# Two query tiles as one seven-product pair job ahead of the gate pair jobs, in a streaming-encoder layer on one core

## The chip, the cores and the metric

The kernel runs on one core of a Trainium2 chip as one program. The metric is the device time of one execution in microseconds, given as a median of runs. A core has five engines that run side by side, each in its own program order: TensorE (PE, matrix products; its weight loads are shown apart as PEld), VectorE (DVE), ScalarE (ACT), GpSimd (POOL) and SyncE (SP, which here only issues DMAs). They wait for one another by semaphores.

## The reference

One layer with four parts: a gated feed-forward, a mixing part with two branches, and a second gated feed-forward, with RMS norms around each. The change lies in the mixing part, whose core is

```python
u = rms_norm(h, mix_pre_g[l])
q, k, v, xr, xg = jnp.split(u @ w_in[l], splits, axis=-1)
xr = causal_conv(xr, conv_w[l], conv_b[l])
hr = rg_lru(xr, rg_a_w[l], rg_a_b[l], rg_x_w[l], rg_x_b[l], lru_lambda[l])
y_a = (hr * jax.nn.gelu(xg)) @ w_lru_out[l]
y_b = swa_sink_attention(q, k, v, attn_sinks[l], bias) @ w_attn_out[l]
g = jax.nn.sigmoid(u @ w_gate[l] + b_gate[l]).reshape(b, s, N_BRANCHES, d)
merged = g[:, :, 0] * y_a + g[:, :, 1] * y_b
```

There are 512 tokens and 1024 channels; q has 1024 columns (16 heads of 64), xg has 1024. `rg_lru` ends in a scan over the tokens; the attention needs q, k and v.

## The kernel before

**Precision by parts.** Every fp32 operand is held as a high part, which ACT makes by a copy into a reduced type, and a low part, the difference that DVE makes. A product is three matmuls: high by high, low by high, high by low. Weights come in by SP's queue as raw tiles of 512 KB; `split_to` or `split2` makes the parts. Tiles come from one pool of 42 slots (`NSLOT`); a tile that is asked for while none is free waits for the last reader of an old one.

**Plain units.** `unit(nm, i)` makes 128 output features for all 512 tokens: `mm_feat` (lines 216 to 227) issues 24 matmuls of 512 columns into one PSUM bank. Its weights are asked for by `get`, which splits two tiles ahead and loads three further ones; this running ahead ends where tiles of pair jobs begin (the set `paired`).

**Pair jobs.** `Pairs` makes two feature tiles at once, by seven products in place of eight (a scheme of Strassen's kind, in Winograd's form). The weights of two tiles are quartered into a11, a12, a21 and a22; POOL makes the sums s1, s2 (in tile S12) and s3, s4 (S34). The inputs' quarter sums t1 to t4 are made once. A job is seven blocks (`mm_s`, lines 485 to 496) of 12 matmuls with 256 columns, over four k-tiles. `prep(m, i)` readies job m's weights in five steps: 0 POOL's sums, 1 the parts of a11 and a12, 2 of s12, 3 of s34, 4 of a22. In `GeluPairs.run` (line 644) the blocks are issued in the order a11, s1, [a22 of the job before], s2, a12, s4, s3; the last job issues a12 after s3, then its own a22. Three banks are used per job: `bu` by a11, s2, s3 and a22, which add up in it with ACT copying the state between them (q1 after a11, line 658; u after s2; v after s3, line 682); `bx` by s1 and s4; `bc` by a12. Preparation of the next job stands between the blocks, as do `last` (the gelu of the quarter that a22 closes), `mult` (line 698, times the scan's result) and `parts` (the high and low parts of the product, yh and yl, inputs of the later `lru` units).

**What sets the order.** Each engine's instructions are laid down by hand in program order. `point()` (line 201) moves a counter on by one; `later(n, fn, rank)` puts work n points ahead, and at each point the work that has come due is issued, lower rank first. `mm_feat` calls `point` twice per unit, each value tile once, `mm_s` once per block. `point(True)` issues all that is still waiting.

**The stage of the change.** In order: units xr 4 to 7 (points 1 to 8), wg 0 to 7 (9 to 24), wk 0 and 1 (25 to 28), four value tiles (29 to 32), wq 0 and 1 (33 to 36), `point(True)`, then four xg pair jobs, then units mixed with the attention's steps (`att_units`, from line 1377 on). Between them stand, by points: the recurrent branch's gates, decay factors (`rg_decay`) and scans (`rg_scan`, line 1133: eight square roots on ACT at `SCAN_AT`, then the scan of tile i on DVE `SCAN_LAG[i]` points later, a product and a scan); the first pair job's preparation (`PREP_AT`, its raw loads and those of the second job at `RAW_AT`, the second job's sums at `PREP_1`). `k_out` (line 1207) takes the keys from PSUM: four ACT copies, two DVE differences, two ACT copies across. `v_out` makes the parts of the values. `q_out` (line 1244) takes a query tile from PSUM: two ACT copies of 64 rows with the scale, then two DVE differences, into a QS tile whose upper rows hold the high part and whose lower rows the low part. `att_s` (line 1278) multiplies QS 2g and 2g + 1 by the keys of group g. `t_spill` writes t1 to t4 to memory through SP's queue, in xg jobs 1 and 2, for a later stage.

Of the kernel before, what the change touches and what calls it, by code (L numbers as in the profile page):

```python
# [13 lines left out]
ALU = mybir.AluOpType  # L14
# [37 lines left out]
def hybrid_layer(ctx: ExitStack, tc: tile.TileContext, a: dict, out: bass.AP):  # L52
# [68 lines left out]
    order += [("wk", 0), ("wk", 1), ("wv", 0), ("wv", 1)]  # L121
    order += [("wq", 0), ("wq", 1)]
    paired.update(range(len(order), len(order) + 8))
    order += [("xg", i) for i in range(8)]

# [71 lines left out]
    def later(n, fn, rank=1):  # L197
        uid[0] += 1
        due.append((now[0] + n, rank, uid[0], fn))
# [29 lines left out]
    def unit(nm, i, **kw):  # L229
        w = get(nm, i)  # L230
        ps = bank("f")
        mm_feat(ps, w, **kw)
        return ps
# [407 lines left out]
    class GeluPairs(Pairs):  # L641


        def run(self, scans, yh, yl, tail, between):
            X, end = self.X, len(self.jobs) - 1
# [5 lines left out]
            for n, (nm, f) in enumerate(self.jobs):  # L651
# [32 lines left out]
                if n == end:  # L684
                    c11()
                gelu(c[:, 0, :])
                if n < end:
# [3 lines left out]

                def last(W=W, bu=bu, c=c):
                    mm_s(W["a22"], X["t4"], bu, True)
                    act.activation(c[:, 1, :256], bu, AF.Gelu_apprx_tanh)
                    gelu(c[:, 1, 256:])

                def mult(c=c, f=f):
                    dve.tensor_tensor(out=c, in0=c, in1=scans[f // 2], op=ALU.mult)

                def parts(c=c):  # L700
                    yh.append(slot([P, 2, SEQ], F32R, name="yh"))
                    yl.append(slot([P, 2, SEQ], F32R, name="yl"))
                    split2(yh[-1], yl[-1], c)
# [441 lines left out]
    X3 = {"b11": uview(0, 0), "b21": uview(1, 0), "b22": uview(1, 1)}  # L1145
    pairs_g = GeluPairs(("xg",), 0, 8, X3)

    def t_hi(key, src):
# [103 lines left out]

    for i in range(2):
        ps = unit("wq", i)
        later(1, lambda i=i, ps=ps: q_out(i, ps))

    yh, yl = [], []
    point(True)
    spills = {1: ("t1", "t2"), 2: ("t3", "t4")}
    pairs_g.run(scans, yh, yl, lambda: split_to(st["split"] + 1), lambda n: [t_spill(key) for key in spills.get(n, ())])  # L1260
    X3 = pairs_g = None
# [211 lines left out]
SCAN_AT = (23,) * 8  # L1473
SCAN_LAG = (1, 2, 3, 4, 5, 6, 7, 8)

T_AT = (3, 4, 5, 6), (4, 5, 6, 7)
RAW_AT = (18, 27)
PREP_AT = (22, 27, 29, 31, 33)
PREP_1 = 30
NSLOT = 42  # L1480
# [70 lines left out]
```

## Time and profile before

| what | value |
|---|---|
| time, median of 3 runs | 1128.34 us (1128.21 to 1128.47) |
| profiled execution, its own time | 1128.54 us |
| its span, first to last instruction | 1126.8 us |
| mean granted TensorE clock | 0.998 |
| HBM read, written | 121.74 MB, 11.53 MB |
| instructions | 18041 |

The profile is of one execution. Its page gives busy times for each engine, the span in 40 slices, the chain of work that ended last, and the costliest groups of instructions. A timeline row has the start, the duration, the engine, the line in the kernel, the operation, out<-in by the program's names, shapes and count, and in brackets the idle time of the engine before it with what ended it. Starts are in us from the span's start.

### The profile page before, as it was taken

To read this page: it belongs to the slowest core of one execution; us is meant where nothing else is said; L and a number is where in the kernel's file an instruction comes from. 1 tells how busy PE (TensorE), PEld (TensorE's weight loads), DVE (VectorE), ACT (ScalarE), POOL (GpSimd) and SP (SyncE) were. 2 spreads that over 40 slices of the span, in tenths; PEclk is the share of its full clock that TensorE was granted. 3 is DMA by queue.
4 is the path that set the end of the run, shared out by engine and by line. 5 is a ranking of instruction groups with operands and counts; after the bars stand their busy time and mean duration, and the time that the engine had idled before them with its cause. 6 is when DMAs were issued, how large, how long until landed. Compare 5 with 4: busy or idle time off the path is not lost.

```text
span 1126.8 us, 18041 instructions
## 1 busy us (share of the span) xinstructions
PE 1118.7 (99%) x7018; PEld 1012.3 (90%) x7018; DVE 833.1 (74%) x1233; ACT 620.8 (55%) x1107; POOL 362.0 (32%) x282
## 2 busy tenths in 40 slices
PE   9999999999999999999999999999999999999997
PEld 8899999988889977899888888889999999998886
DVE  5889989886436998887778867767898777975313
ACT  7755555574325788756655654456555555564211
POOL 0044344200000523232656663000866566700000
PEclk9999999999999999999999999999999999999999
DMA  9226563265213553156132336521333232264101
GB/s 346 96 86 148 133 133 113 76 224 164 98 57 139 164 116 105 38 165 247 57 94 75 131 112 225 180 101 38 113 105 93 103 113 87 87 203 167 38 20 56
DMA packets 40310, 136.54 MB, mean 121 GB/s; under 512 B 4880, under 2 KB 6800, under 8 KB 40224
## 3 DMA queue, kind: packets, MB, share of 16 engines
q1 hardware_dynamic: 36432, 123.28, 32.4%
q0 software_dynamic: 3504, 11.58, 5.2%
q8 instruction: 55, 0.90, 0.3%
q10 hardware_dynamic: 288, 0.52, 0.1%
q14 instruction: 31, 0.25, 0.1%
HBM read 121.74 MB, written 11.53 MB: 118 GB/s over the span
## 4 chain that ended last, share of the span: by engine, by line
PE 99%; DVE 0%; issue 0%; DVEq 0%; POOL 0%; ACT 0%; POOLq 0%
PE c L492 13%; PE c L493 13%; PE c L494 13%; PE f L223 9%; PE f L224 9%; PE f L225 9%; PE acc L243 8%; PE acc L241 8%; PE acc L242 8%; PE pt L1329 1%; PE s L1293 1%; PE s L1292 1%; PE tr L333 1%; PE o L1345 1%; PE o L1346 1%; PE f L847 1%
## 5 line engine op out<-in xcount | busy, mean ns | idle before, releaser
L493 PE MATMUL c<-uT,wlo 128*128 128x256 f32 x516 | 146.0, 283 | 0.0
L494 PE MATMUL c<-uT,whi 128*128 128x256 f32 x516 | 146.0, 283 | 0.0
L492 PE MATMUL c<-uT,whi 128*128 128x256 f32 x516 | 146.0, 283 | 0.0
L493 PE MATMUL c<-Xh,wlo 128*128 128x256 f32 x504 | 142.7, 283 | 0.0
L492 PE MATMUL c<-Xh,whi 128*128 128x256 f32 x504 | 142.7, 283 | 0.0
L223 PE MATMUL f<-uT,whi 128*128 128x512 f32 (+1 forms) x392 | 140.6, 359 | 0.0
L224 PE MATMUL f<-uT,wlo 128*128 128x512 f32 (+1 forms) x392 | 139.1, 355 | 0.0
L225 PE MATMUL f<-uT,whi 128*128 128x512 f32 (+1 forms) x392 | 139.0, 355 | 0.0
L241 PE MATMUL acc<-whi,hT 128*128 128x512 f32 x352 | 137.1, 390 | 0.0
L242 PE MATMUL acc<-wlo,hT 128*128 128x512 f32 x352 | 137.0, 389 | 0.0
L243 PE MATMUL acc<-whi,hT 128*128 128x512 f32 x352 | 136.9, 389 | 0.0
L214 DVE TENSOR_TENSOR wlo<-S,whi 128x1024 fp32r<-128x1024 f32 x86 | 126.7, 1473 | 7.5 <-POOL OL L1365 4.5
L494 PE MATMUL c<-Xl,whi 128*128 128x256 f32 x456 | 129.0, 283 | 0.0
L213 ACT ACTIVATE whi<-S 128x1024 fp32r<-128x1024 f32 x86 | 88.3, 1054 | 23.7 <-DVE S L539 22.0
L493 PEld LDWEIGHTS c<-uT,wlo 128*128 128x128 f32 x516 | 99.0, 192 | 0.2
L492 PEld LDWEIGHTS c<-uT,whi 128*128 128x128 f32 x516 | 99.0, 192 | 0.2
L494 PEld LDWEIGHTS c<-uT,whi 128*128 128x128 f32 x516 | 99.0, 192 | 0.0
L492 PEld LDWEIGHTS c<-Xh,whi 128*128 128x128 f32 x504 | 96.8, 192 | 0.3 <-issue 0.3
L493 PEld LDWEIGHTS c<-Xh,wlo 128*128 128x128 f32 x504 | 96.7, 192 | 0.1
L494 PEld LDWEIGHTS c<-Xl,whi 128*128 128x128 f32 x456 | 87.5, 192 | 0.0
L223 PEld LDWEIGHTS f<-uT,whi 128*128 128x128 f32 x392 | 74.1, 189 | 11.6 <-issue 1.6
L225 PEld LDWEIGHTS f<-uT,whi 128*128 128x128 f32 x392 | 74.1, 189 | 10.5
(380 smaller groups left out, 2858.5 us busy)
## 6 DMA issues: line engine op xcount, KB each, us to landing
raw_w2a<-in_w2a_dram SPq DMA_DIRECT2D x22, 512.0 KB, 4.0
raw_w1b<-in_w1b_dram SPq DMA_DIRECT2D x22, 512.0 KB, 4.3
raw_w3b<-in_w3b_dram SPq DMA_DIRECT2D x22, 512.0 KB, 4.2
raw_w2b<-in_w2b_dram SPq DMA_DIRECT2D x22, 512.0 KB, 4.0
raw_w3a<-in_w3a_dram SPq DMA_DIRECT2D x21, 512.0 KB, 4.5
raw_w1a<-in_w1a_dram SPq DMA_DIRECT2D x20, 512.0 KB, 4.3
raw_wg<-in_wg_dram SPq DMA_DIRECT2D x16, 512.0 KB, 3.8
raw_xr<-in_xr_dram SPq DMA_DIRECT2D x8, 512.0 KB, 3.9
```

Source lines behind the costliest of these rows:

```text
L213: act.activation(hi, src, AF.Copy)
L214: dve.tensor_tensor(out=lo, in0=src, in1=f32(hi), op=ALU.subtract)
L223: pe.matmul(ps[:, c0:c1], wh[:, s], h_, start=k == 0, stop=False)
L224: pe.matmul(ps[:, c0:c1], wl[:, s], h_, start=False, stop=False)
L225: pe.matmul(ps[:, c0:c1], wh[:, s], l_, start=False, stop=k == KT - 1)
L241: pe.matmul(acc[n], x[:, 0, c], wh[:, s], start=first, stop=False)
L242: pe.matmul(acc[n], x[:, 0, c], wl[:, s], start=False, stop=False)
L243: pe.matmul(acc[n], x[:, 1, c], wh[:, s], start=False, stop=last)
L333: pe.transpose(ps[:, k * P : (k + 1) * P], hg[:, kk * P : (kk + 1) * P], ident)
L492: pe.matmul(ps, wh[:, s], xh, start=first, stop=False, skip_group_check=True)
L493: pe.matmul(ps, wl[:, s], xh, start=False, stop=False, skip_group_check=True)
L494: pe.matmul(ps, wh[:, s], xl, start=False, stop=k == 3, skip_group_check=True)
```

## The change

The two query tiles wq 0 and wq 1 are no longer plain units: they are the first of now five jobs of `pairs_g`, as job 0, and the xg jobs are jobs 1 to 4. `q_pair` takes a query tile from the job's result `c` in SBUF and lays out QS as `q_out` does, with the high part of the second head on the rows that it has in `c`. Query tile 0 is taken in job 1, where an xg job has `mult`; query tile 1 is put 21 points after job 1's `parts`, which is the point at the end of the s3 block of job 4. The wq job has no gelu and no parts.

`point(True)` ahead of the jobs is gone, so work that is due later goes on into them. `SCAN_LAG` changes from 1 to 8 in steps of one to 1, 1, 2, 3, 4, 5, 8, 37: the scan of tile 1 comes one point earlier, and tiles 2 to 5 likewise, tile 6 one point later, and tile 7 at point 60, the first block of job 4. `RAW_AT`, `PREP_AT` and `PREP_1` are earlier by up to three points; they now ready the wq job first, and xg job 0's sums second. The spills are in jobs 2 and 3, the same xg jobs as before.

```diff
@@ the order of the weights
-    order += [("wq", 0), ("wq", 1)]
-    paired.update(range(len(order), len(order) + 8))
-    order += [("xg", i) for i in range(8)]
+    paired.update(range(len(order), len(order) + 10))
+    order += [("wq", 0), ("wq", 1)] + [("xg", i) for i in range(8)]
...
@@ GeluPairs.run
-        def run(self, scans, yh, yl, tail, between):
+        def run(self, scans, yh, yl, q_pair, tail, between):
...
-                gelu(c[:, 0, :])
+                if nm == "xg":
+                    gelu(c[:, 0, :])
...
-                def last(W=W, bu=bu, c=c):
+                def last(W=W, bu=bu, c=c, nm=nm):
                     mm_s(W["a22"], X["t4"], bu, True)
+                    if nm == "wq":
+                        act.activation(c[:, 1, :256], bu, AF.Copy)
+                        return
                     act.activation(c[:, 1, :256], bu, AF.Gelu_apprx_tanh)
                     gelu(c[:, 1, 256:])
 
-                def mult(c=c, f=f):
+                def mult(c=c, f=f, nm=nm):
+                    if nm == "wq":
+                        q_pair(f, c[:, 0, :])
+                        return
                     dve.tensor_tensor(out=c, in0=c, in1=scans[f // 2], op=ALU.mult)
 
-                def parts(c=c):
+                def parts(c=c, f=f, nm=nm):
+                    if nm == "wq":
+                        later(21, lambda: q_pair(f + 1, c[:, 1, :]))
+                        return
...
     pairs_g = GeluPairs(("xg",), 0, 8, X3)
+    pairs_g.jobs.insert(0, ("wq", 0))
+    pairs_g.k0 -= 2
...
-    for i in range(2):
-        ps = unit("wq", i)
-        later(1, lambda i=i, ps=ps: q_out(i, ps))
+    def q_pair(i, c):
+
+        q_ = slot([P, 2, SEQ], F32R, name="QS")
+        sc = HD ** -0.5
+        for j, r0 in ((0, 0), (1, 64)):
+            act.activation(q_[r0 : r0 + 64, j, :], c[r0 : r0 + 64, :], AF.Copy, scale=sc)
+        for j, r0 in ((0, 0), (1, 64)):
+            dve.scalar_tensor_tensor(
+                out=q_[64 - r0 : 128 - r0, j, :], in0=c[r0 : r0 + 64, :], scalar=sc, in1=f32(q_[r0 : r0 + 64, j, :]),
+                op0=ALU.mult, op1=ALU.subtract)
+        QS[i] = q_
 
     yh, yl = [], []
-    point(True)
-    spills = {1: ("t1", "t2"), 2: ("t3", "t4")}
-    pairs_g.run(scans, yh, yl, lambda: split_to(st["split"] + 1), lambda n: [t_spill(key) for key in spills.get(n, ())])
+    spills = {2: ("t1", "t2"), 3: ("t3", "t4")}
+    pairs_g.run(scans, yh, yl, q_pair, lambda: split_to(st["split"] + 1), lambda n: [t_spill(key) for key in spills.get(n, ())])
...
@@ the times in points
-SCAN_LAG = (1, 2, 3, 4, 5, 6, 7, 8)
+SCAN_LAG = (1, 1, 2, 3, 4, 5, 8, 37)
...
-RAW_AT = (18, 27)
-PREP_AT = (22, 27, 29, 31, 33)
-PREP_1 = 30
+RAW_AT = (18, 25)
+PREP_AT = (22, 26, 27, 28, 31)
+PREP_1 = 29
```

## The prediction, as it was put on record

> **What bounds the kernel now.** I read the page first: its engine line and its chain of waits.
>
> ```profile
> span 1126.8 us, 18041 instructions
> PE 1118.7 (99%) x7018; PEld 1012.3 (90%) x7018; DVE 833.1 (74%) x1233; ACT 620.8 (55%) x1107; POOL 362.0 (32%) x282
> PE 99%; DVE 0%; issue 0%; DVEq 0%; POOL 0%; ACT 0%; POOLq 0%
> ```
>
> The chain that ended last runs through PE for 99% of the span, so only two things can move the time: how long PE's stream of matmuls is, and whether PE must wait. The busy time of a matmul is modelled and overlaps the next, so I take PE's work from the distance between starts, in the timeline of PE: the first matmul of wq 0, the first of xg job 0, of xg job 1 and of xg job 2.
>
> ```profile
> 473.61 0.40 PE L223 MATMUL f<-uT,whi 128*128 128x512 f32 x1
> 484.52 0.28 PE L492 MATMUL c<-uT,whi 128*128 128x256 f32 x1
> 493.15 0.28 PE L492 MATMUL c<-uT,whi 128*128 128x256 f32 x1
> 503.23 0.28 PE L492 MATMUL c<-uT,whi 128*128 128x256 f32 x1
> ```
>
> The two wq units take 484.52 - 473.61 = 10.91 us for 48 matmuls of 512 columns (0.227 each). A pair job takes 503.23 - 493.15 = 10.08 us for 84 matmuls of 256 columns (0.120 each; 1.44 us per block of 12). The first job's last block (a22) runs inside the next job, so a job's own six blocks take 493.15 - 484.52 = 8.63.
>
> Then the windows view (us; PE, PEld, DVE, ACT, POOL busy; clock; DMA) for the first xg job and the stretch where DVE is fullest:
>
> ```profile
> 484.50:493.15 8.65, 8.65 (x73) 8.63 (x72) 6.60 (x9) 5.17 (x8) 2.55 (x2) 1.00 0.17 67
> 503.23:513.31 10.08, 10.08 (x86) 10.08 (x85) 9.99 (x7) 6.13 (x12) 6.56 (x4) 1.00 0.81 274
> ```
>
> PE is busy throughout and the granted clock is 1.00. DVE has 2.05 us left in the first job and 0.09 in the third, so what the change adds to DVE or ACT must be placed in time.
>
> **The stream.** Removed: 48 matmuls, 10.91 us. Added: 84, 10.08 us. Sum: -0.83 us, the only change in PE's work.
>
> By the Trainium skill (TensorE: Matmul & The Clock Gate, "Back-to-back issue gap") an isolated matmul costs N/2.4 + 2.5 ns: an estimate from it is 84 x 109 against 48 x 216 ns, or -1.2 us. The rows above show 120 and 227 ns, so the rows stay.
>
> **Work before the job.** The job's weights are needed 10.91 us earlier than those of xg job 0 are now. Named by points (a counter that every half unit, value tile or block moves on), PE reaches point 32 at 473.61, where the job begins; point 28 four value tiles earlier (24 matmuls of 0.120 each: 462.1) and point 24 two units (5.45 each) before that: 451.2. DVE and ACT run in program order, so I laid DVE's new order out with these rows, from the timelines of DVE, ACT and POOL:
>
> ```profile
> 450.40 0.68 DVE L1139 TENSOR_TENSOR ig<-xc_t,ig 128x512 f32<-128x512 f32 x1
> 454.61 0.69 DVE L1139 TENSOR_TENSOR ig<-xc_t,ig 128x512 f32<-128x512 f32 x1
> 456.48 0.66 DVE L1139 TENSOR_TENSOR ig<-xc_t,ig 128x512 f32<-128x512 f32 x1
> 458.32 1.20 DVE L179 TENSOR_TENSOR wlo<-raw_wv,whi 128x1024 fp32r<-128x1024 f32 x1
> 459.43 1.40 DVE L1213 TENSOR_TENSOR KS<-f,KS 64x512 fp32r<-64x512 f32 x2
> 469.82 1.41 DVE L1213 TENSOR_TENSOR KS<-f,KS 64x512 fp32r<-64x512 f32 x2
> 474.92 1.79 DVE L1139 TENSOR_TENSOR ig<-xc_t,ig 128x512 f32<-128x512 f32 x1
> 483.68 0.68 DVE L214 TENSOR_TENSOR w<-raw_xg,w 128x512 fp32r<-128x512 f32 x1
> 469.87 1.30 POOL L543 TENSOR_TENSOR S<-raw_xg 128x512 f32<-128x512 f32 x1 [25.32 <-DVE wlo L179]
> 473.88 2.28 POOL L539 TENSOR_TENSOR S<-raw_xg,raw_xg 128x512 f32<-128x512 f32 x1
> 455.34 1.05 ACT L178 ACTIVATE whi<-raw_wv 128x1024 fp32r<-128x1024 f32 x1
> 470.54 1.36 ACT L1216 ACTIVATE KS<-KS 64x512 fp32r<-64x512 f32 x2 [3.63 <-DVE KS L1213]
> 473.29 0.64 ACT L213 ACTIVATE V<-v 128x256 fp32r<-128x256 f32 x2
> 476.26 0.62 ACT L213 ACTIVATE w<-raw_xg 128x512 fp32r<-128x512 f32 x1
> 486.15 0.38 ACT L658 ACTIVATE ct<-c 128x256 f32<-128x256 f32 x1 [0.24 <-PE c L494]
> ```
>
> A scan step is 456.48 - 454.61 = 1.87 us on DVE, a low part of 1024 columns 459.43 - 458.32 = 1.11, the key parts of one tile 1.40. The new order, from 450.40 as before:
>
> - point 24, scans 0 and 1, then wv 0's low part: 455.3
> - point 25, scan 2: 457.1
> - point 26, a11's low part, scan 3, wv 1's: 461.3
> - point 27, key parts of tile 0: 462.7. ACT now copies the key parts across (1.4) and makes s12's high part (1.05), so DVE idles till 465.0 at the latest; s12's low part, scan 4: 468.0
> - point 28, s34's low part, scan 5: 471.0
> - point 29, key parts of tile 1: 472.4
>
> So a11, s12 and s34 are there at about 458, 466 and 469, for use at 473.61, 475.05 and 479.37; a22 follows at about 475, for use at 485.13. PE does not wait for weights: 9 us and more of cover. That wq 0 and 1's four splits go (on DVE 2 x 1.11) is part of this relief. The gain of it on the path is nothing.
>
> What is late next is a copy on ACT. After the key parts ACT must copy them across (1.36), take four value tiles (0.32 each) and a22's high part (0.62), and only then read the first block's bank (L658). That bank is written again at the third block, 2.88 us after the job's start, 476.49. From 472.4 ACT needs 1.4 + 1.3 + 0.6 = 3.3 and is free at 475.7; the read takes 0.38: 476.1. Margin 0.4 us. Against it: POOL's sums for the next job now start when their slots are free, which is earlier since DVE is less behind. Beside POOL an L1139 took 1.79 in place of 0.68, 1.1 us more. Bounds for the delay of the key parts: 0, and two such steps, 2.2 us. PE's stall is then between 0 and 2.2 - 0.4 = 1.8 us. I take 0: the idle time at point 27 takes up what POOL costs before it, and one late step costs 0.7 at most.
>
> By the Trainium skill (SBUF - State Buffer, "SBUF: two separate sides") a DVE operation with two SBUF inputs and a GpSimd one exclude each other for a whole instruction. The stretched L1139 beside L539 agrees (1.79 and 2.28). By that rule each meeting costs DVE at most one POOL operation, which is the bound above.
>
> **The last job.** Scan 7 (1.87 on DVE) moves to this job's first block, and the second query tile (two ACT copies, two DVE operations) behind its s3 block. Rows now, of the last xg job; the changed ones should stand 0.83 earlier:
>
> ```profile
> 484.39 1.39 DVE L1250 SCALAR_TENSOR_TENSOR QS<-f,QS 64x512 fp32r<-64x512 f32 x2
> 484.72 1.20 ACT L1248 ACTIVATE QS<-f 64x512 fp32r<-64x512 f32 x2 [4.24 <-PE f L225]
> 516.62 0.68 DVE L214 TENSOR_TENSOR w<-raw_xg,w 128x512 fp32r<-128x512 f32 x1
> 518.55 1.23 DVE L698 TENSOR_TENSOR cc<-cc,ig 128x1024 f32<-128x1024 f32 x1 [1.25 <-ACT cc L650]
> 519.81 1.06 ACT L213 ACTIVATE yh<-cc 128x1024 fp32r<-128x1024 f32 x1 [0.15 <-DVE cc L698]
> 520.78 1.05 ACT L178 ACTIVATE whi<-raw_wq 128x1024 fp32r<-128x1024 f32 x1
> 522.15 0.39 ACT L682 ACTIVATE ct<-c 128x256 f32<-128x256 f32 x1 [0.33 <-PE c L494]
> 523.39 0.28 PE L492 MATMUL c<-Xh,w 128*128 128x256 f32 x1
> 525.78 1.23 DVE L179 TENSOR_TENSOR wlo<-raw_lru,whi 128x1024 fp32r<-128x1024 f32 x1 [1.65 <-ACT whi L178]
> 527.58 0.22 PE L1292 MATMUL s<-KS,QS 128*128 128x128 f32 x1
> 529.26 1.22 DVE L214 TENSOR_TENSOR yl<-cc,yh 128x1024 fp32r<-128x1024 f32 x1 [1.13 <-ACT yh L213]
> 531.54 0.35 DVE L1298 CUSTOM_DVE_ANT_0 P<-s,BT,vec 128x128 f32<-128x128 f32 x1
> ```
>
> Now the copy L682 ends at 522.54 and the a22 block, which writes its bank again, starts at 523.39: 0.85 us to spare. In the new times: DVE ends a22's low part at 516.47, scan 7 at 518.3, the product L698 at 519.5 (0.6 later than 518.95); so yh runs 519.55 to 520.6, wq 2's high part to 521.6, the two query copies to 522.7, and L682 to 523.1. PE wants its bank at 522.56: a stall of 0.5. Bounds: 0 if both are hidden (without the scan's 0.6 L682 would end at 522.5), 0.9 if the copies take 0.4 more. I take 0.4.
>
> The query tile's DVE half ends at about 524.3 and its first reader (L1292) comes at 526.8: 2.5 us of cover. The last product's low part moves from 530.5 to about 531.4; the lru unit uses it in its last quarter, after 534. The scores (L1298) start about 1 us later, behind which POOL's factors follow; they have the wait for the bias tile as cover.
>
> **The rest at nothing.** The xg jobs between hold what they held; in xg job 0's place as second job, the first query tile (1.4 on DVE, 1.2 on ACT) takes the place of no work, in a job where DVE had 2.05 us left. The loads on SP's queue change places (wq at point 18, xg at 25), the spills stay with the same xg jobs, POOL's sums come one job more often in the same rhythm. Their cover is a lead of a whole job; the slot that the pair's result and scan 7 hold longer could cost one block's wait, 1.44 us, if that lead is used up.
>
> **Sum** against the profiled execution (1128.54, its span 1126.8 and 1.7 around it; 0.20 over the median): -0.83 + 0 + 0.4 = -0.43 us. From the median 1128.34 that is 1127.9.
>
> **Rivals.**
> 1. *Slower: the first bank read on ACT comes late* (job 1's third block). It decides from key parts later than 472.8, and turns the sum positive from 473.2 on. For it: the wait of 3.63 us at L1216, ACT already hangs on DVE there, and POOL's 1.1 us per meeting. Against it: idle time at point 27. Price up to 1.8: 1127.9 + 1.3 = 1129.2 for a middling delay, 1129.7 at the bound.
> 2. *All late pieces are hidden*: 1128.34 - 0.83 = 1127.5. For it: 0.85 us to spare at L682 now. Against it: query copies stand ahead of it in order.
> 3. *Slots run short* and one job's weights come a block late: 1127.9 + 1.4 = 1129.3. For it: POOL's L543 waits for slots in each job. Against it: PE never waits for them now.
> 4. *The pair form costs more per matmul than now* and the stream gains nothing: 84 x 0.130 = 10.9, so 1128.3 + 0.4 = 1128.7. All 28 blocks of the four xg jobs take 1.44, which speaks against it. The Trainium skill (TensorE: Matmul & The Clock Gate, "Back-to-back issue gap") also gives sustained figures, 81 ns at 128 columns and 131 at 512; halfway in columns an estimate is 98, 84 x 98 against 48 x 131 ns, or +1.9 us. The rows contradict both figures.
>
> **Chances.** Forecast (stalls of 0.2 to 0.7) 0.42; all hidden 0.28; ACT late 0.18; slots 0.08; dearer matmuls 0.01; something unseen, mostly slower, 0.03. The range takes in rival 2 with the scatter of 0.13 either way and most of rivals 1 and 3: 1127.3 to 1129.2. What this measurement tells from no change is about 0.2%, 2.26 us. A gain of that size would need three times the stream's saving: 0.02. A loss of it needs stalls of 3.1 us, so both rivals 1 and 3 at their bounds or something unseen: 0.07. Within 0.2%: 0.91.
>
> **What would show it.** Right: six blocks of 1.44 from about 473.6, the second job at 482.25, the first attention score at about 527.1 in place of 527.58. Wrong: a gap before the third block of the wq job (rival 1), before a block that waits for S weights (3), a step other than 1.44 (4); no gap before the last job's a22 block would make the 0.4 wrong. A stall outside 450 to 540 us would be one that I have not seen.

## The result, and the profile after

| what | before | after |
|---|---|---|
| time, median in the same series (us) | 1128.40 (6 runs) | 1133.58 (6 runs, 1132.26 to 1134.10) |
| ratio to before, 95% interval | | 1.0041 [1.0028, 1.0054] |
| profiled execution, its span (us) | 1128.54, 1126.8 | 1133.62, 1131.6 |

The change makes the kernel slower by 0.3 to 0.5%. Of the six executions after, the four with a mean granted clock of 0.996 or 0.997 took 1133.54 to 1134.10 us, and the two with 0.998 took 1132.26 and 1132.63. The forecast was 1127.9 us, its range ended at 1129.2. The page of the changed kernel begins with the same three lines that were shown of before (span, busy times, chain of waits):

```profile
span 1131.6 us, 18135 instructions
PE 1120.0 (99%) x7054; PEld 1014.5 (90%) x7054; DVE 842.2 (74%) x1238; ACT 624.3 (55%) x1114; POOL 369.6 (33%) x286
PE 92%; DVE 4%; ACT 2%; issue 1%; DVEq 0%; POOL 0%; ACTq 0%; POOLq 0%
```

The chain, 99% on PE before, now leaves PE for 8% of the span. Where, the timeline of PE tells: the first value tile, the first matmul of job 0, then the rows around each wait, the first matmul of job 1, and the first attention score.

```profile
461.56 0.28 PE L1247 MATMUL v<-whi,uT 128*128 128x256 f32 x1
473.08 0.28 PE L491 MATMUL c<-uT,whi 128*128 128x256 f32 x1
...
475.84 0.28 PE L493 MATMUL c<-wlo,whi 128*128 128x256 f32 x1
476.57 0.39 PE L491 MATMUL c<-Xh,whi 128*128 128x256 f32 x1 [0.45 <-ACT ct L657]
476.79 0.28 PE L492 MATMUL c<-Xh,wlo 128*128 128x256 f32 x1
...
482.42 0.28 PE L491 MATMUL c<-uT,whi 128*128 128x256 f32 x1
...
506.81 0.28 PE L493 MATMUL c<-wlo,w 128*128 128x256 f32 x1
509.40 0.38 PE L491 MATMUL c<-Xh,whi 128*128 128x256 f32 x1 [2.31 <-ACT ct L657]
509.62 0.28 PE L492 MATMUL c<-Xh,wlo 128*128 128x256 f32 x1
...
526.68 0.28 PE L493 MATMUL c<-uT,whi 128*128 128x256 f32 x1
526.87 0.39 PE L491 MATMUL c<-Xh,w 128*128 128x256 f32 x1
527.09 0.28 PE L492 MATMUL c<-Xh,w 128*128 128x256 f32 x1
...
531.15 0.22 PE L1310 MATMUL s<-KS,QS 128*128 128x128 f32 x1
```

A stall is read as the distance from the last matmul before it to the second after it, less two pitches of 0.12: 476.79 - 475.84 - 0.24 = 0.71 before job 0's third block, 509.62 - 506.81 - 0.24 = 2.57 before job 3's s2 block, 527.09 - 526.68 - 0.24 = 0.17 before the last job's own a22. Each of the first two waits for the copy q1 (L657), which takes a11's bank away.

The windows view shows what followed the second stall (us; PE, PEld, DVE, ACT, POOL busy; granted clock; DMA share and GB/s), in the 3.3 us that begin a block's length behind the wait:

```profile
510.60:513.90 3.30, 3.30 (x18) 3.30 (x17) 2.24 (x2) 2.80 (x5) 0.00 (x0) 0.50 1.00 407
```

There are 18 matmuls at a granted clock of 0.50. A run below has the same wait without a fall of the clock, and 30 matmuls in as long a window: 12 x 0.12 = 1.44 us more. That is also about the distance between the two groups of executions above.

The first value tile of the kernel before:

```profile
462.10 0.28 PE L1236 MATMUL v<-whi,uT 128*128 128x256 f32 x1
```

From the first value tile to the first score PE took 527.58 - 462.10 = 65.48 us before and 531.15 - 461.56 = 69.59 after: 4.11 more. The terms found: -0.83 (the stream) + 0.71 + 2.57 + 1.44 + 0.17 = 4.06. From the first score to the end of the span it is 1126.8 - 527.58 = 599.2 before and 1131.6 - 531.15 = 600.4 after: 1.2 more, in the attention. The part ahead of the values came out 0.54 shorter in this execution.

**Why q1 is late in job 3.** The timelines of DVE, POOL (the first of its four sums for the last job) and ACT of the changed kernel:

```profile
503.12 2.11 DVE L213 TENSOR_TENSOR yl<-cc,yh 128x1024 fp32r<-128x1024 f32 x1
505.15 2.31 DVE L213 TENSOR_TENSOR wlo<-S,whi 128x1024 fp32r<-128x1024 f32 x1
507.39 1.48 DVE L682 TENSOR_TENSOR cc<-ct 128x256 f32<-128x256 f32 x1
...
502.85 1.30 POOL L542 TENSOR_TENSOR S<-raw_xg 128x512 f32<-128x512 f32 x1 [3.77 <-PE c L493]
...
508.96 0.38 ACT L657 ACTIVATE ct<-c 128x256 f32<-128x256 f32 x1 [4.14 <-DVE cc L682]
```

The job's first block is long done, yet ACT idles 4.14 us ahead of q1, because q1's tile `ct` waits for DVE's addition L682 of the job before. There are two ingredients, and the kernel before has less of both at the same place:

```profile
502.34 1.21 DVE L214 TENSOR_TENSOR yl<-cc,yh 128x1024 fp32r<-128x1024 f32 x1
503.47 2.32 DVE L214 TENSOR_TENSOR wlo<-S,whi 128x1024 fp32r<-128x1024 f32 x1
505.71 1.51 DVE L683 TENSOR_TENSOR cc<-ct 128x256 f32<-128x256 f32 x1
...
505.88 0.38 ACT L658 ACTIVATE ct<-c 128x256 f32<-128x256 f32 x1 [1.02 <-DVE wlo L214]
```

First, the slot. Before, the copy into the new `ct` starts right behind the low part that reads S34, the operation ahead of the addition; now it starts right behind the addition, which reads the `ct` of the job before. So, by what releases it, the new `ct` has now got that tile's slot, and waits one DVE operation longer. Second, DVE itself: POOL's sums for the last job stretch DVE's rows in both kernels, but the changed kernel has a set of sums in one job more, and DVE enters this job later. Its low part ends at 507.46, 0.53 behind the time at which PE wanted the s2 block (506.93); before, it ended at 505.79, and the s2 block came three blocks (a11, s1, a22) behind 503.23, at 507.55: 1.76 ahead. That is 2.3 us of DVE's lateness and 1.4 us (507.46 to 508.87) for the slot. The lateness has two parts: DVE starts yl's low part 503.12 - 502.61 = 0.51 behind the job's first matmul (502.61), where before it was 503.23 - 502.34 = 0.89 ahead, so it enters 1.40 later; and POOL, which begins as the job does, now stretches this row too, to 2.11 in place of 1.21.

### The profile page after: what moved, and what is told of

It reads as the page before. It is cut to its first block, busy times and chain, and to the rows that moved or that the text cites. A ratio compares the mean times of both kernels' runs of the same rounds, so it can differ in the third digit from the quotient of the medians.

```text
span 1131.6 us, 18135 instructions
## 1 busy us (share of the span) xinstructions
PE 1120.0 (99%) x7054; PEld 1014.5 (90%) x7054; DVE 842.2 (74%) x1238; ACT 624.3 (55%) x1114; POOL 369.6 (33%) x286
## 4 chain that ended last, share of the span: by engine, by line
PE 92%; DVE 4%; ACT 2%; issue 1%; DVEq 0%; POOL 0%; ACTq 0%; POOLq 0%
PE c L491 13%; PE c L492 13%; PE c L493 13%; PE acc L241 8%; PE acc L240 8%; PE acc L242 8%; PE f L222 7%; PE f L223 7%; PE f L224 7%; PE pt L1347 1%; DVE wlo L178 1%; ACT P L1324 1%; PE tr L332 1%; DVE P L1316 1%; PE o L1364 1%
## 5 line engine op out<-in xcount | busy, mean ns | idle before, releaser
L491 PE MATMUL c<-uT,whi 128*128 128x256 f32 x528 | 150.0, 284 | 0.0
L492 PE MATMUL c<-uT,wlo 128*128 128x256 f32 x528 | 149.9, 284 | 0.0
L493 PE MATMUL c<-uT,whi 128*128 128x256 f32 x528 | 149.9, 284 | 0.0
L491 PE MATMUL c<-Xh,whi 128*128 128x256 f32 x516 | 146.5, 284 | 2.8 <-ACT ct L657 2.8
L492 PE MATMUL c<-Xh,wlo 128*128 128x256 f32 x516 | 146.3, 283 | 0.0
L213 DVE TENSOR_TENSOR wlo<-S,whi 128x1024 fp32r<-128x1024 f32 x88 | 131.0, 1489 | 7.3 <-ACT whi L212 3.3
L222 PE MATMUL f<-uT,whi 128*128 128x512 f32 (+1 forms) x376 | 134.4, 357 | 0.7 <-DVE o L1378 0.7
L223 PE MATMUL f<-uT,wlo 128*128 128x512 f32 (+1 forms) x376 | 132.8, 353 | 0.0
L224 PE MATMUL f<-uT,whi 128*128 128x512 f32 (+1 forms) x376 | 132.8, 353 | 0.0
L491 PEld LDWEIGHTS c<-uT,whi 128*128 128x128 f32 x528 | 102.0, 193 | 0.1
L492 PEld LDWEIGHTS c<-uT,wlo 128*128 128x128 f32 x528 | 101.9, 193 | 0.1
L493 PEld LDWEIGHTS c<-uT,whi 128*128 128x128 f32 x528 | 101.9, 193 | 0.0
L222 PEld LDWEIGHTS f<-uT,whi 128*128 128x128 f32 x376 | 71.1, 189 | 11.9 <-issue 1.4
L224 PEld LDWEIGHTS f<-uT,whi 128*128 128x128 f32 x376 | 71.1, 189 | 9.9
```

Of the source, the lines that this page charges most:

```text
L213: dve.tensor_tensor(out=lo, in0=src, in1=f32(hi), op=ALU.subtract)
L222: pe.matmul(ps[:, c0:c1], wh[:, s], h_, start=k == 0, stop=False)
L223: pe.matmul(ps[:, c0:c1], wl[:, s], h_, start=False, stop=False)
L224: pe.matmul(ps[:, c0:c1], wh[:, s], l_, start=False, stop=k == KT - 1)
L491: pe.matmul(ps, wh[:, s], xh, start=first, stop=False, skip_group_check=True)
L492: pe.matmul(ps, wl[:, s], xh, start=False, stop=False, skip_group_check=True)
```

## The experiments

All times are medians of several runs beside runs of the kernel before (1128.1 to 1128.3 in each series). Edits are against the changed kernel unless said. "Value to score" is the distance of the first matmuls of v and s on PE, and "score to end" that from s to the end of the span: 65.48 and 599.2 before, 69.59 and 600.4 after.

**The slot.** Two `ct` tiles, asked for once and used in turn:

```diff
+            cts = [slot([P, 4, 256], name="ct") for _ in range(2)]
             for n, (nm, f) in enumerate(self.jobs):
-                tmp = slot([P, 4, 256], name="ct")
+                tmp = cts[n % 2]
```

> The changed kernel, with two ct tiles used in turn by the jobs in place of a new one for each. Theory S (the new job's first bank copy waits only because its ct tile got the slot of the job before's ct tile, whose last reader is DVE's late addition): the wait of 2.3 us before job 3's s2 block and the half clock after it go, some 4.3 us less than the changed kernel, 1129.3 us or a ratio of 1.001 to the kernel before; the wait of 0.45 us in job 0 stays. Rival D (DVE has too much work in jobs 1 to 3, and PE would wait for it in one way or another): the wait only moves to a weight or another copy, at least 2 us of it stay, 1131.5 us or more.

Measured: 1131.41 us, ratio 1.0025 [1.0015, 1.0035], 2.1 us above S's figure and at the edge of D's. Job 3 has no wait, and the clock stays up. But the last job loses 0.27 in its s1 block, and at its own a22, where 0.17 was lost, now 525.10 - 522.95 - 0.24 = 1.91:

```profile
522.95 0.28 PE L493 MATMUL c<-uT,whi 128*128 128x256 f32 x1
524.88 0.38 PE L491 MATMUL c<-Xh,w 128*128 128x256 f32 x1 [1.65 <-ACT ct L682]
525.10 0.28 PE L492 MATMUL c<-Xh,w 128*128 128x256 f32 x1
...
521.24 1.06 ACT L212 ACTIVATE yh<-cc 128x1024 fp32r<-128x1024 f32 x1 [1.91 <-DVE cc L705]
...
523.15 1.26 ACT L1270 ACTIVATE QS<-cc 64x512 fp32r<-64x512 f32 x2
524.44 0.38 ACT L682 ACTIVATE ct<-c 128x256 f32<-128x256 f32 x1
```

This is the prediction's chain for the last job (scan 7, product, yh, high part, two query copies, then v), with DVE late at its start. The run does not test the slot alone. With two tiles asked for at the start, other tiles get other slots as well, and POOL's first sum for the last job begins 1.7 us later:

```profile
504.56 2.21 POOL L542 TENSOR_TENSOR S<-raw_xg 128x512 f32<-128x512 f32 x1 [5.23 <-DVE yl L213]
```

So yl's and S34's low parts of job 3 take 1.21 each in place of 2.11 and 2.31, and the product later in that job 2.31. The slots decide where the wait falls, and 2.2 of the 5.2 us; DVE's lateness stays and shows at the next place that has no cover.

The counterpart on the kernel before, with one `ct` tile for all its xg jobs:

```diff
+            ct = slot([P, 4, 256], name="ct")
             for n, (nm, f) in enumerate(self.jobs):
-                tmp = slot([P, 4, 256], name="ct")
+                tmp = ct
```

> The kernel before, with one ct tile for all four xg jobs in place of a new one for each, so that each job's first bank copy must wait for the last DVE addition of the job before. Theory S: in xg job 2 that addition ended at 507.2 where PE writes the bank again at 507.55, and the copy takes 0.38 behind it, so a wait of 0.1 to 0.5 us appears there: 1128.4 to 1129. Rival D: DVE's work is the same, so no change, 1128.3.

Measured: 1128.48, ratio 1.0 [0.999, 1.0009], no wait of PE. The time does not tell S from D, but the wait that S expected is not there. The ACT rows in the third xg job show that a tile which is kept is waited for by its parts: q1's copy goes through, and only the one of q5 waits for the addition. In the changed kernel q1's copy, into a new tile in the old slot, waits for that addition, which does not read q1.

```profile
504.38 0.38 ACT L659 ACTIVATE ct<-c 128x256 f32<-128x256 f32 x1
506.83 0.38 ACT L661 ACTIVATE ct<-c 128x256 f32<-128x256 f32 x1 [2.06 <-DVE cc L684]
```

**The spread.** Scan 7 back to its place behind scan 6:

```diff
-SCAN_LAG = (1, 1, 2, 3, 4, 5, 8, 37)
+SCAN_LAG = (1, 1, 2, 3, 4, 5, 8, 8)
```

> The changed kernel with the scan of tile 7 at lag 8 (point 31) in place of 37, so that one slot is free earlier and DVE has 1.9 us more before job 0's weights for job 1. Theory S: the ct tiles of jobs 2 and 3 get other slots, the wait in job 3 goes, 1129.3 us within 0.8. Rival D: DVE's work in jobs 1 to 3 is what it was, plus what is put off from before; the time stays at 1133 or more.

Measured: 1132.79, ratio 1.0041 [1.0026, 1.0056], between the two theories' figures. In job 3 q1's copy starts behind the low part (508.92), as before the change, yet the s2 block waits for it again (0.78), since DVE is late; and in job 2 the s1 block waits for its low part:

```profile
495.34 0.38 PE L492 MATMUL c<-Xh,wlo 128*128 128x256 f32 x1 [1.11 <-DVE wlo L213]
```

And the whole spread undone (`SCAN_LAG` 1 to 8 as in before, the second query tile at once in job 1: `q_pair(f + 1, c[:, 1, :])` in place of `later(21, ...)`):

> The changed kernel with nothing spread: scans at lags 1 to 8 as before, the second query tile taken in job 1 at once (two more ACT copies and DVE operations there, 1.4 us of DVE). Theory S: other slots for ct, no wait in job 3, 1129 to 1130 us, with the wait in job 0 longer than 0.45 us, up to 2, since DVE's scans stand ahead of the keys. Rival D: job 1 is fuller still, so PE waits in jobs 2 or 3 for 3 us or more, 1133.5 or more.

Measured: 1134.48, ratio 1.0055 [1.004, 1.007], as rival D has it. The long wait for q1, now 3.28, moves to job 2, job 1's first block waits 0.83 for its low part, and job 3 has no wait. Score to end falls to 599.2, the figure of before. So the spread is of use in the jobs, and it is what costs the attention its 1.2 us.

**POOL's sums for the last job.** Left out, by memsets of the same tiles:

```diff
             if i == 0:
                 e = eng or pool
+                if self.jobs[m] == ("xg", 6):
+                    e.memset(s12, 0.0)
+                    e.memset(s34, 0.0)
+                    return
```

> The changed kernel, but POOL's four sums for the last job are two memsets of the same tiles (the last job then multiplies zeros in place of s1 to s4; the slots and the order are as in the changed kernel). Theory C: the wait in job 3 (2.6 us of PE, and 1.4 more at half clock) needs two things, a ct tile in the slot of the job before and a DVE that runs late beside POOL's sums for the job after next. With POOL's additions gone, the DVE operations of 505 to 511 us fall back from 1.5 to 2.3 us to their own 0.4 to 1.2, the addition after v ends about 2 us earlier, and the wait in job 3 falls from 2.6 to under 0.6 with no half clock: 1129.4 to 1130.4. Rival S alone: the slot decides whatever POOL does, the wait stays above 2 us: 1133 or more. Rival M: a memset on POOL holds DVE up as an addition does, then nothing changes either; its rows would show it.

Measured: 1129.73, ratio 1.0013 [1.0004, 1.0022]; value to score 65.54. The windows row of job 3:

```profile
502.40:512.50 10.10, 10.10 (x87) 10.10 (x86) 8.92 (x13) 8.33 (x14) 1.91 (x2) 1.00 0.69 238
```

The changed kernel's row for that job, with the same 13 operations of DVE:

```profile
502.40:516.40 14.00, 11.69 (x86) 11.48 (x85) 12.83 (x13) 8.05 (x14) 6.99 (x4) 0.88 0.67 238
```

Beside POOL's four additions these take 12.83 - 8.92 = 3.91 us longer; by their rows, the four that stretch take 7.65 in place of 3.55. POOL's two memsets, at 503.19 and 504.75 (0.95 each), stretch nothing, so rival M is out. In the timeline of the run without sums the addition after v (L686 here) ends 2.7 us earlier than L682 in the changed kernel:

```profile
504.61 1.22 DVE L213 TENSOR_TENSOR wlo<-S,whi 128x1024 fp32r<-128x1024 f32 x1
505.75 0.42 DVE L686 TENSOR_TENSOR cc<-ct 128x256 f32<-128x256 f32 x1
...
506.26 0.38 ACT L661 ACTIVATE ct<-c 128x256 f32<-128x256 f32 x1 [1.08 <-DVE cc L686]
```

The slot is still the bad one here, and with DVE in time it costs nothing.

That leaves open whether POOL's additions hurt as neighbours or DVE merely has too much in that job. So the same sums go to DVE itself:

```diff
-                    self.prep(n + 2, 0)
+                    self.prep(n + 2, 0, dve if n == 2 else None)
```

> The changed kernel with one edit: the four sums for the last job are DVE's own, not POOL's (the output stays the reference's). Theory X: what makes DVE late in job 3 is that its operations with two SBUF operands stretch beside POOL's additions, some 4.3 us in that stretch; the sums themselves are four operations of 0.7 us on DVE, so 2.7 us more work and 4.3 less stretch leave DVE 1.6 us earlier, and the addition after v, which now stands ahead of the sums and not beside them, some 2 us earlier: the wait in job 3 under 0.5, the last job's between 0.2 and 1.4, 1129.7 to 1131.0. Rival W: DVE has too much work there however it is shared out, 2.7 us more make the wait longer: 1133.5 or more.

Measured: 1130.00, ratio 1.0017 [1.0007, 1.0026]: 3.6 us less than the changed kernel (the half clock is gone with the wait), with four more operations on the fuller engine.

```profile
502.40:512.60 10.20, 10.20 (x87) 10.20 (x86) 10.13 (x14) 7.11 (x13) 0.00 (x0) 1.00 0.69 265
```

That row has 14 operations of DVE, and none of POOL. In its timeline the addition after v ends at 506.21, and the four sums follow, from 506.73 on (0.68 to 0.69 each):

```profile
505.79 0.42 DVE L682 TENSOR_TENSOR cc<-ct 128x256 f32<-128x256 f32 x1
```

Four sums take 4 x 0.68 = 2.7 us of DVE, less than the 3.9 us that they cost it from POOL; and the addition L682 stands ahead of them. Rival W is out: it is the neighbour. DVE enters job 3 as late as in the changed kernel (yl's low part starts 503.52 - 503.00 = 0.52 behind the job's first matmul), and PE does not wait there. So DVE's late entry alone is not enough; and before the change, with DVE 1.40 earlier and the other slot, the sums alone were not either.

**The stall in job 0.** Three runs on its cause. First, DVE's 1.1 us low part of a11 and a12 by ACT and an accumulating transfer (`split_dma(ra, ...)` in place of `both(ra)` for job 0):

> The changed kernel, but the low half of job 0's a11 and a12 is made by a second ACT copy and an accumulating transfer in place of DVE's 1.1 us subtraction. Theory: the first stall (0.71 us at 476.6) is DVE's lateness at the key parts, so it goes (0 to 0.1), and the rest stays: 1132.6 to 1133.2. Rival: the key parts are late for ACT's sake (it now has 1.05 more to do before them), and the stall stays or grows: 1133.6 to 1134.5.

Measured: 1133.40, ratio 1.0045 [1.0029, 1.0062], the stall unchanged (0.72). DVE comes to s12's low part 0.48 earlier, at 463.35, and goes on from it at 465.34 in place of 465.26: what it saved ahead of POOL's sums it loses beside them, and the theory is out. Second, the sums for job 1 left out, by memsets as above for `("xg", 0)`:

> The changed kernel, but POOL's four sums for job 1 are two memsets of the same tiles (job 1 then multiplies zeros in place of s1 to s4). Theory P: DVE's lateness at the second tile's keys (472.3 us) comes from these sums, beside which its operations of 463 to 469 us take 1.5 to 2.2 us in place of 0.7 to 1.2; with them gone the keys end 2 to 2.8 us earlier and the 0.7 us stall before job 0's third block is gone (under 0.1); job 3 keeps its wait: 1132.5 to 1133.2. Rival: the chain of ACT and DVE there is as late without POOL, the stall stays: 1133.4 or more.

Measured: 1132.55, ratio 1.0039 [1.0024, 1.0054], the stall gone. DVE's scan 4 and key parts in the changed kernel, with POOL's first sum, then the same two rows of DVE in this run:

```profile
467.08 2.20 DVE L1149 TENSOR_TENSOR_SCAN ig<-xc_t,ig 128x512 f32<-128x512 f32 x1
...
472.28 1.41 DVE L1224 TENSOR_TENSOR KS<-f,KS 64x512 fp32r<-64x512 f32 x2
...
461.58 1.29 POOL L542 TENSOR_TENSOR S<-raw_xg 128x512 f32<-128x512 f32 x1 [17.56 <-PE f L223]
```

```profile
465.85 1.23 DVE L1153 TENSOR_TENSOR_SCAN ig<-xc_t,ig 128x512 f32<-128x512 f32 x1
...
470.09 1.41 DVE L1228 TENSOR_TENSOR KS<-f,KS 64x512 fp32r<-64x512 f32 x2
```

The key parts come 2.2 us earlier. Third, a22's parts behind job 0's second block (`PREP_AT`'s last entry 31 to 34, the job's weights kept until then), which takes 0.63 us out of ACT's order ahead of q1:

> The changed kernel with the parts of job 0's a22 made three points later, behind the second block of the job. Theory: the first bank read of job 0 (0.7 us stall) stands in ACT's order behind the key copies, the values and a22's high part (0.63 us); with the last of these gone the read ends 0.6 earlier and the stall falls to about 0.1, the rest as before: 1132.6 to 1133.3. Rival: the values' copies on ACT wait for DVE and the read moves by less than 0.2: 1133.4 to 1134.

Measured: 1133.22 (5 runs), ratio 1.0041 [1.0027, 1.0055]; the stall is under 0.1. Its profiled execution, 1135.18, is the longest of the five, with a front 2.0 us longer; the stall's own 0.7 is within the scatter of these medians.

**The attention.** The second query tile at the end of the last job's s1 block (`later(17, ...)`):

> The changed kernel with the second query tile four points earlier, at the end of the last job's s1 block instead of its s3 block. Theory Q: the attention's loss (from the first score to the end 600.4 us in place of 599.2) is the tile's two DVE operations, 1.4 us ahead of the addition after v, on which the first scores hang through the gelu, the product and the low parts; it falls to 599.2 to 599.6 and the waits in front of the scores' blocks go; the stall in job 3 stays: 1132.4 to 1133.0. Rival: scan 7 is the cause, the loss stays at 1.2: 1133.4 or more.

Measured: 1132.75, ratio 1.004 [1.0025, 1.0055]. Score to end fell only to 600.1, against the theory's 599.2 to 599.6, and the last job waits 0.86 for v. The time is within the expected span for another reason: the same wait of 2.57 us in job 3 was followed by full clock.

```profile
511.10:514.40 3.30, 3.30 (x30) 3.30 (x29) 2.24 (x2) 2.80 (x5) 0.00 (x0) 1.00 1.01 413
```

Both pieces earlier, with two `ct` tiles (`later(14, ...)`, which falls at the end of job 3's s4 block, not of its s3 block as the expectation says, and scan 7's lag 9):

> Two ct tiles used in turn, the second query tile seven points earlier (end of the s3 block of job 3) and scan 7 one point behind scan 6. Theory L: the last job's wait (1.9 us once the slots are out of the way) and about 1 us in the attention come from these late pieces; both go (last job under 0.2, first score to end 599.2 to 599.4): 1128.7 to 1129.7, what is left being the stall at the first bank read. Rival D: DVE has no room for them anywhere, a block waits for a low part instead, as in job 2 with scan 7 alone moved (1.4 us): 1130.5 to 1132.

Measured: 1131.46, ratio 1.003 [1.0019, 1.0041]. Score to end is 599.3, as theory L has it; but job 3 loses 1.97 and the last job 0.85, the time that rival D gives. Job 3's s3 block waits for u's copy, which stands on ACT behind a high part; and that waits 4.89 us for DVE's low part of a22 (L213), late beside POOL's sums. The second wait, 0.59 for v, stands behind the two query copies, which are now ahead of yh and v in ACT's order:

```profile
513.42 0.39 PE L491 MATMUL c<-Xh,whi 128*128 128x256 f32 x1 [1.71 <-ACT ct L665]
...
511.46 1.06 ACT L212 ACTIVATE whi<-raw_xg 128x1024 fp32r<-128x1024 f32 x1 [4.89 <-DVE w L213]
```

What the attention hangs on is how far the first score operation on DVE stands behind the first score on PE. These two rows of the changed kernel give 536.53 - 531.15 = 5.38; before it was 531.54 - 527.58 = 3.96. Some 34 us behind the first score stands the one wait of PE that the profile shows from there to the end, at the unit that follows an o product. Rows of the changed kernel, then the same unit before, without a wait:

```profile
536.53 0.35 DVE L1316 CUSTOM_DVE_ANT_0 P<-s,BT,vec 128x128 f32<-128x128 f32 x1
...
565.49 0.47 PE L222 MATMUL f<-uT,whi 128*128 128x512 f32 x1 [0.75 <-DVE o L1378]
```

```profile
560.48 0.40 PE L223 MATMUL f<-uT,whi 128*128 128x512 f32 x1
```

From the first score to this unit it is 565.49 - 531.15 = 34.34 us, and 560.48 - 527.58 = 32.90 before: 1.44 more. (The last four rows of the table are runs that follow below.)

| run | behind by (us) | score to that unit (us) | score to end (us) |
|---|---|---|---|
| before | 3.96 | 32.90 | 599.2 |
| before, one ct | 3.98 | 32.90 | 599.6 |
| spread undone | 4.15 | 33.13 | 599.2 |
| both pieces earlier | 4.25 | 33.22 | 599.3 |
| query tile in s1 | 4.91 | 33.87 | 600.1 |
| two ct | 5.18 | 34.27 | 600.3 |
| after | 5.38 | 34.34 | 600.4 |
| scan 7 early alone | 5.37 | 34.34 | 600.8 |
| addition from PSUM | 4.29 | 33.27 | 599.7 |
| sums of jobs 3 and 4 on DVE | 4.48 | 33.43 | 600.6 |
| the same, two ct | 4.93 | 33.88 | 600.2 |
| query tile in s4 | 4.83 | 33.79 | 600.0 |

What the first score operation is late beyond 4.0 us has come out by that unit, nearly one for one. Score to end follows only roughly: behind the unit the executions differ by up to 1.1 us, which these rows do not explain. Scan 7 early alone changes nothing here, the query tile four points earlier alone takes 0.5 of the 1.4: each delays the same chain. The query tile's two DVE operations (1.40) stand ahead of the last job's additions, scan 7 ahead of the product before them, and from the additions the gelu, the last product, its low part and the scores follow in DVE's order.

**Relief of DVE by other means.** Two `ct` tiles, both pieces earlier, and the low halves of a11 and a12 of three jobs by accumulating transfer. The edit names wq 0, xg 0 and xg 2, which are jobs 0, 1 and 2, not 0, 1 and 3 as the expectation says:

> As the run before, and the low half of a11 and a12 of jobs 0, 1 and 3 by ACT copy and accumulating transfer, which takes 1.1 us (2.3 beside POOL) from DVE in each. Theory: DVE then has the room, no stall over 0.3 us is left, and the stream's -0.83 shows: 1127.4 to 1128.0. Rival A: ACT (1.05 more a job) or the transfers come late instead: 1128.5 to 1131.

Measured: 1136.15, ratio 1.0071 [1.0056, 1.0086], as rival A but dearer: job 1's first block waits 4.18 us for the transfer, and job 2's 0.92. POOL issues job 1's transfer soon after ACT's copy for it (479.14), so POOL's order does not hold it up; PE goes on 7.9 us behind the issue.

```profile
479.44 0.89 POOL L160 DMA_DIRECT2D wlo<-in_xg_dram  x1 [10.78 <-ACT ct L668]
...
487.34 0.58 PE L492 MATMUL c<-uT,wlo 128*128 128x256 f32 x1 [4.18 <-DMA wlo<-in_xg_dram]
```

The addition after v taken from PSUM, with the other moves:

```diff
-                act.activation(v, bu, AF.Copy)
-                dve.tensor_tensor(out=c[:, 1, 256:], in0=v, in1=q5, op=ALU.add)
+                if n == end:
+                    act.activation(v, bu, AF.Copy)
+                dve.tensor_tensor(out=c[:, 1, 256:], in0=v if n == end else bu, in1=q5, op=ALU.add)
```

> The changed kernel with two ct tiles in turn, job 0's a22 parts three points later, the second query tile at the end of the last job's s1 block, scan 7 right behind scan 6, and the addition after v read from PSUM by DVE (no ACT copy to v but in the last job, no second SBUF operand, so that POOL cannot hold it up: 0.4 us in place of 1.5 in three jobs). Theory: DVE is relieved by some 3 us between 485 and 512 us, job 3's and the last job's waits fall under 0.4 each, the first under 0.15: 1127.6 to 1129.0, at best 0.7 under the kernel before. Rival D: the s2 or a22 block now waits for DVE's read of the bank, which comes late beside POOL: 1129.5 to 1132.

Measured: 1131.47, ratio 1.0033 [1.002, 1.0046]: rival D. The addition is short now (0.41, at 507.87), but it comes as late as it did, behind low parts stretched beside POOL, and PE waits for the bank, 0.59 us in job 1 and 2.19 in job 3:

```profile
508.34 0.39 PE L491 MATMUL c<-Xh,w 128*128 128x256 f32 x1 [2.19 <-DVE cc L686]
```

**Putting it together.** The last job's sums on DVE and a22's parts later (the run that the text calls the run before is the one with the sums on DVE):

> The run before with job 0's a22 parts three points later as well. If both causes stand on their own, the first stall (0.7 us) goes and nothing else moves: 0.7 below the run before, 1129.0 to 1130.3. Rival: POOL's and DVE's times shift and the gain comes out in a later wait: no lower than the run before.

Measured: 1129.38, ratio 1.0011 [1.0001, 1.002]: the two causes add up, 0.6 of 0.7. Then the sums of jobs 3 and 4 on DVE, a22's parts later, the query tile in the last job's s1 block and scan 7 in job 2 (lag 25), with `ct` as it is and with two:

> Sums of jobs 3 and 4 on DVE, job 0's a22 parts three points later, the second query tile at the end of the last job's s1 block, scan 7 at point 48 in job 2. Theory: DVE has room for the scan in job 2 once no addition of POOL's stretches it; the first score follows its block by 4.3 us or less, and with it the attention's loss falls under 0.4: 1127.8 to 1129.3. Rival: DVE's own sums of job 3 wait for their slots and hold up what stands behind them: 1129.5 to 1132.

> The run before with two ct tiles in turn. If a wait on a ct slot is left there, it goes: 1127.6 to 1129.0; if none is, the same time within 0.3; rival: the slot that is held longer delays a raw tile or a split, 0.5 to 2 us more than the run before.

Measured: 1129.96, ratio 1.0016 [1.0007, 1.0026], with 0.66 lost again in job 3 to the slot that `ct` gets (q1's copy waits for a low part till 506.61); and 1129.07, ratio 1.001 [1.0001, 1.0019], without it. Both lie above the theory's span, the second by 0.07. The first score stands 4.48 and 4.93 behind, not the 4.3 or less of the first expectation, and a loss in the attention stays. Last, the query tile in the last job's s4 block (`later(20, ...)`):

> The candidate with two ct tiles, with the second query tile at the end of the last job's s4 block instead of s1: its two ACT copies then fall into ACT's 1.5 us of waiting for the product, and its two DVE operations (1.4 us) come behind the product instead of ahead of it. Theory: the first score follows its block by about 4.2 us instead of 4.9 and the attention's loss of 1.0 goes to 0.2 or less: 1128.0 to 1128.5, level with the kernel before or up to 0.4 under it. Rival: the copies push yh and with it v, and the last job waits 0.5 to 1.5 us: 1128.8 to 1130.

Measured: 1128.80 (11 runs), ratio 1.0006 [0.9997, 1.0015]. Value to score is 527.08 - 462.12 = 64.96, so here the saving is seen: 65.48 - 0.83 + 0.26 of one small stall = 64.91.

```profile
462.12 0.28 PE L1250 MATMUL v<-whi,uT 128*128 128x256 f32 x1
527.08 0.22 PE L1313 MATMUL s<-KS,QS 128*128 128x128 f32 x1
```

The first score operation stands 4.83 us behind (531.91 - 527.08), not the 4.2 that was expected, and the attention takes the gain back: 33.79 - 32.90 = 0.89 up to the unit that waits. The time lies above the theory's span, at the lower edge of the rival's, but the rival's wait in the last job is not there. No version came out faster than the kernel before.

## Why the prediction was wrong

- **The stream, -0.83: right.** Job 0's own six blocks take 482.42 - 473.08 = 9.34 us, which is 8.63 and the stall of 0.71; the last candidate shows the saving whole.
- **Weights in time: right.** No block of job 0 waits for weights.
- **The first bank read, taken at 0: measured 0.71**, inside its bounds of 0 to 1.8. It is rival 1, at its place (the prediction counts the wq job as job 1 there). The failed step is "the idle time at point 27 takes up what POOL costs before it". POOL began its sums at 461.58, not at 469.87 as before, and stretched three operations (to 1.51, 1.78 and 2.20) behind that idle time as well. The key parts ended at 473.69 and not at 472.4.
- **The last job, 0.4: measured 0.17**, with PE made late by job 3. With DVE in time it is 0.17 as well (the sums left out), with DVE late 1.91. The chain was right; its size depends on where DVE stands, which was not carried over from the jobs ahead of it.
- **"The rest at nothing": wrong, and the step that failed the forecast.** It put the jobs between at 0, for a sum of -0.43; job 3 alone cost 2.57 and, in this execution, 1.44 at half clock. "The xg jobs between hold what they held" counts instructions. The prediction's own row for the third xg job had DVE busy 9.99 of 10.08 us, so a job of that kind has no room to make up what DVE is late on entering it, and that was 1.40 us. The lead of a whole job was weights' lead; the tile that ran out of cover was `ct`, which the prediction did not look at. Rival 3 had the kind right (a slot) but the wrong tile and one block's price.
- **The attention: not seen.** "They have the wait for the bias tile as cover" failed: scores that DVE begins 1.4 us later behind PE cost 1.44 us up to the unit that waits for o, 1.2 us at the end. It is outside 450 to 540 us, which the prediction named as what it had not seen.
- **Rival 4, the dearer pair form: rightly given next to no chance.** A block takes 1.44 us in the wq job too. In its working, 98 ns is not halfway between the two figures that it cites but a third of the way, as 256 columns lie between 128 and 512; nothing hangs on it.

That POOL's neighbouring additions are a cause of both stalls in the jobs is shown by leaving them out and, for the larger, by giving them to DVE. The larger came with DVE's late entry into job 3 and with the slot; before, without these two, such sums cost PE nothing. How much each of the two adds is read from the rows, not tested apart. Where the late entry comes from stays open: POOL's one set of sums more and the first query tile's two DVE operations (1.41 at 489.31, in job 1) both stand ahead of it. What follows between the first score operation and the wait for o was not followed step by step; that the one sets the other rests on the table.

## What to carry to other kernels

When work is put ahead of a stretch in which an engine is full, cost the stretch again from the state in which the engine enters it: a job with 0.1 us to spare passes lateness on, and it comes out at the first wait without cover. For each buffer that is taken from a pool, look at whose slot it gets, since a new tile waits for every reader of the old one, where a tile that is kept is waited for part by part. And an operation given to an idle engine is not free if it slows the full one: four sums on POOL cost DVE 3.9 us, on DVE itself 2.7.

## What the runs showed of the hardware

Five profiled executions have a wait of PE of 2.31 to 2.33 us in job 3. In four of them (the changed kernel, a11 by transfer, no sums for job 1, a22's parts later) some 3.3 us at a granted clock of 0.50 follow, in one (query tile in s1) full clock. After waits of 3.28 and 4.18 us the clock fell as well; after waits of 1.65, 1.71 and 2.19 us it did not. So a wait of some 2.3 us can cost 1.44 us more than itself. The Trainium skill (TensorE: Matmul & The Clock Gate, "Part 1: The HAM clock gate") describes a gate that halves the clock after an idle window of about 3.4 us, with windows that run free of the program. The length of the slow stretch and its coming and going agree with that; that 2.3 us of idleness are enough does not agree with a whole idle window.

DVE operations with two SBUF operands grow by up to 1.1 us beside POOL's additions (a low part of 1024 columns from 1.22 to 2.31), also the scan (1.23 to 2.20). The Trainium skill (SBUF - State Buffer, "SBUF: two separate sides") has this as an exclusive lock on a shared port. It says that this holds against GpSimd operations that read SBUF only, and the runs agree: beside POOL's memsets (503.19 and 504.75 in the run without sums), which read nothing, the low parts keep their own length (1.22).
